# Down projection of a gated feed-forward: where its raw weight tiles lie and in which order its loads are issued

## The chip, the core and the metric

The kernel runs on one core of a Trainium2 chip. Its time is the device time of one execution in microseconds, and the value of a kernel is the median of its runs. A profile is one further execution with its own time.

Five engines work beside each other, each on its own instruction stream in a fixed order: TensorE (PE; its weight loads are listed as PEld), VectorE (DVE), ScalarE (ACT), GpSimd (POOL) and SyncE (SP). Here SP only issues DMAs. An issue that must wait, for a semaphore of another engine or for the landing of an earlier DMA, holds all issues behind it on the same engine. GpSimd issues a few DMAs too, on a queue of its own.

## The reference, cut to what matters

The reference is one layer of a streaming encoder: a mixer with three kinds of recurrent heads, then a convolutional feed-forward, each between two norms, for a prompt of 1024 tokens and a sample of 32. The change touches the feed-forward:

```
def conv_ffn(xn, buf, w_up, conv_w, conv_b, w_down):
    up = xn @ w_up                                   # 1024 -> 2 * 2816
    up, buf = causal_dwconv(up, buf, conv_w, conv_b) # 3 taps along time
    gate, val = jnp.split(up, 2, axis=-1)
    return (jax.nn.gelu(gate, approximate=True) * val) @ w_down, buf
...
        h, ffn_buf = conv_ffn(rms_norm(x, g_ffn_pre[l]), states[6][l], ...)
        x = x + rms_norm(h, g_ffn_post[l])
```

All of it is in 32-bit floats.

## The kernel before

**Products.** Each 32-bit operand is split into a high part (a cast by ScalarE, L93) and a remainder (a subtraction by VectorE, L94); a product is three matmuls, high by high, high by low and low by high (`mm3`, L87 to L90). Both feed-forward projections are done as seven block products instead of eight (Strassen-like sums of blocks, called p1 to p7 and P1 to P7).

**Up projection.** `up_all` (L1483) goes over NF = 22 feature tiles f of 128. For each, `up_block` makes gate and value columns for all tokens in two buffers `uu`, and `up_finish` (L1411) applies the three taps, the gelu and the product of both halves, and stores the gated tile, 128 x 1024, to the DRAM tensor `h_d[f]` (L1424, issued by SP). The last product of the last tile multiplies S3 by T3. The operands T2, T3 and T4 and the buffers y, uu and the kept products lie in pools of the right side of the on-chip memory that are closed after it (L1959 to L1962).

**Down projection.** `down_all` (L1613) then computes the seven products in the order P2, P1, P4, P6, P5, P7, P3. Each `run` (L1627) goes over NP = 11 steps p. P2 pairs rows `h_d[11+p]` with the raw weight tile `w_dn[11+p]`, and P1 rows `h_d[p]` with `w_dn[p]`. A step of P2 or P1 casts and splits one half of the row tile (`P2h`, `P1h`; four buffers) and of the raw tile (`P2w`, `P1w`; seven buffers) and does 12 matmuls into four banks. After steps 3, 7 and 9 `sample_products` (L1604) multiply the sample's rows by the raw tiles of steps 0 to 3, 4 to 7 and 8 to 10.

**Its loads.** `down_raw` (L1555) loads a raw tile, 128 x 1024 floats, 512 KB. It deals P2's and P1's tiles, in the order in which they are asked for, to nine buffers: two of a pool that the up projection used (`praw[0]`), five of the pool `ph` on the left side, opened when the last up tile begins (`freed`, L1929), and two of the pool p11 (`praw[2]`). So P2's tiles 0 and 1 take the first two, 2 to 6 the next five, 7 and 8 those of p11, and P2's 9 and 10 and P1's 0 and 1 come again to the buffers of P2's 0 to 3, which the sample products after step 3 read last. `load_h` (L1575) loads a row tile, also 512 KB; all 22 keep their own bytes to the end, rows 11 to 21 in `ph`, rows 0 to 10 in p11. `freed` asks for P2's raws 0 to 3 and rows 11 to 13; the rest is asked for by `rows_of` (L1686), which is called after each step: in P2 rows 14 to 21 after steps 0 to 7 and rows 0 to 5 after steps 5 to 10; in P1 rows 6 to 10. A raw tile from 4 on is asked for when its step's operands are made.

**Where p11 lies.** p10, with the accumulators CA, CB and the output norm's gain `gp`, and p11 are opened on the right side after the up projection's pools close. In p11 tiles lie in the order in which they are first asked for: row 0 at byte 124544 of each partition, row 1 at 128640, the two raw buffers at 132736 and 136832, rows 2 to 10 from 140928. The three y buffers of `up_finish` lay at 127232, 131328 (which holds the last gated tile) and 135424; T3's two parts from 139520 to 155904, then T2 and T4. A tile waits for the readers and writers of the tiles whose bytes it takes.

**What sets the order.** The framework's scheduler orders each engine's instructions by program order, as far as what they depend on has been scheduled. `with tc.issue_after(x)` puts an instruction behind x on the same engine's queue, with no semaphore. `behind["SP"]` holds the raw load that was traced last; `load_h` is put behind it.

Of the kernel before, what the change touches and what calls it, by code (L numbers as in the profile page):

```python
# [8 lines left out]
F32 = mybir.dt.float32  # L9
# [3 lines left out]
AF = mybir.ActivationFunctionType  # L13
# [5 lines left out]
SEQ = 1024  # L19
# [3 lines left out]
NF = DFF // 128  # L23
# [55 lines left out]
def body(ctx: ExitStack, tc: tile.TileContext, a: dict):  # L79
    nc = tc.nc  # L80
    act, dve, pool, pe, sp = nc.scalar, nc.vector, nc.gpsimd, nc.tensor, nc.sync
# [41 lines left out]
    h_d = dr.tile([NF, 128, SEQ], F32, name="h_d")  # L123
# [115 lines left out]
    cols_of, dcs_of, behind = {}, {}, {}  # L239
# [1171 lines left out]
    def up_finish(py, f, uu):  # L1411

        ys = []
        for i, j in enumerate((f, NF + f)):
            u = uu[i][:, 2:]
            y = py.tile([128, SEQ], F32, tag="y", name=f"y{j}", bufs=3)
            behind["POOL"] = pool.tensor_copy(fhalo[:, j, :], u[:, SEQ - 2:SEQ])  # L1417
            act.activation(y, u, AF.Identity, scale=fconv[:, j, 2:3], bias=fconv[:, j, 3:4])  # L1418
            for s in range(2):
                dve.scalar_tensor_tensor(y, uu[i][:, s:s + SEQ], fconv[:, j, s:s + 1], y, op0=ALU.mult, op1=ALU.add)  # L1420
            ys.append(y)
        act.activation(ys[0], ys[0], AF.Gelu_apprx_tanh)
        dve.tensor_tensor(ys[0], ys[0], ys[1], op=ALU.mult)
        sp.dma_start(h_d[f], ys[0])  # L1424

    def up_samples():

# [55 lines left out]
    def up_all(pw_, W0, X, uus, py, freed, ahead, begun):  # L1483
# [4 lines left out]
        for f in range(NF):  # L1488
# [3 lines left out]
            for s in (0, 1) if f == 0 else (None,):  # L1492
                if s != 0:
                    blk = up_block(pw_, f, s, W[f], X, uu)
                    next(blk)
                    next(late, None)
                    m = (2 * f + (1 if s is None else s) - 3) * len(SUMS) // 34
                    while len(summed) < min(m, len(SUMS)):
                        sum_weights(*SUMS[len(summed)])
                        summed.append(m)  # L1500
                    if f:
                        up_finish(py(), f - 1, uus[(f - 1) % len(uus)])
                        W.pop(f - 1)
                    next(blk)
                    if f == NF - 1:
                        freed()
                else:
                    blk = begun
                if s != 0 and f + 1 < NF:
                    ops = up_operands(f + 1, raw.pop(f + 1))  # L1510
                    W[f + 1] = next(ops)
                    for _ in ops:
                        pass
                yield
                if f:
                    next(rounds, None)
                next(blk)
                late = blk
                if f > len(UGROUPS) * (len(VISITS) + 1):
                    next(rounds, None)  # L1520
                yield
        for _ in rounds:
            pass
        ahead()
        next(late, None)
        up_finish(py(), NF - 1, uus[(NF - 1) % len(uus)])

    praw, ph, EARLY = [], [], 3

    NP = NF // 2  # L1530
# [21 lines left out]
    wraws = {}  # L1552
    VISITS_D = {3: range(4), 7: range(4, 8), NP - 2: range(8, NP)}

    def down_raw(kind, p):  # L1555

        key = (kind, p if kind in ("P1", "P2") else p // 2)
        if key in wraws:
            return
        n = len(wraws) % (9 if kind in ("P1", "P2") else 7)  # L1560
        pool_, bufs = (praw[0], 2) if n < 2 else (ph[0], 5) if n < 7 else (praw[2], 2)
        r = pool_.tile([128, 2, 512], F32, tag="raw", name=f"wr{kind}_{p}", bufs=bufs)
        if kind in ("P1", "P2"):
            f = p + NP * (kind == "P2")
            behind["SP"] = sp.dma_start(r.rearrange("p j n -> p (j n)"), a["w_dn"][f])
        else:
            n = min(2, NP - p)
            src = a["w_dn"][NP + p:NP + p + n, :, 512:].rearrange("f p n -> p f n") if kind == "P3" else \
                ws_d[{"P5": 0, "P7": 1, "P6": 2, "P4": 3}[kind]][:, p:p + n, :]
            behind["SP"] = sp.dma_start(r[:, :n, :], src)  # L1570
        wraws[key] = r

    hts = {}

    def load_h(pool_, f):  # L1575
        hts[f] = pool_.tile([128, SEQ], F32, name=f"ht{f}")
        with tc.issue_after(behind["SP"].ins):
            sp.dma_start(hts[f], h_d[f])

    def ablk(i, k, p):  # L1580
        h = hts[p + NP * k]
# [9 lines left out]
    def down_operands(ph, kind, p, early=False):  # L1591
        down_raw(kind, p)
        late = tc.issue_after(kept["w"].ins) if kind == "P1" and p else ExitStack()
        with late:
            h = halves_of(ablk(*ASRC[kind], p), f"{kind}h{p}", ph, "hop", 4)
        wp = (ph, "hop", 4) if early else (praw[1], "op", 7)
        if kind in ("P1", "P2"):
            r = wraws[kind, p]
            w = halves_of(r[:, 0], f"{kind}w{p}", *wp)
        else:  # L1600
            w = halves_of(wraws[kind, p // 2][:, p % 2], f"{kind}w{p}", *wp)
        return h, w

    def sample_products(ps, k, qs):  # L1604

        with tc.issue_after(behind["PE"].ins):
            for q in qs:
                for j in range(2):
                    r = 64 * (q % 2) + DEC * j
                    pe.matmul(ps[r:r + DEC], smp_h[:, q + NP * k, :], wraws["P2" if k else "P1", q][:, j],  # L1610
                              start=q < 2, stop=q >= NP - 2)

    def down_all(ph, pc, begun, late):  # L1613
# [1 line left out]
        CA = pc.tile([128, 4, 2, 512], F32, name="ca")  # L1615
        CB = pc.tile([128, 4, 2, 512], F32, name="cb")
        gp = pc.tile([128, 1024], F32, name="gp")
        sp.dma_start(gp, a["grows"][1:2, :].broadcast_to([128, 1024]))
        act.activation(gp[:, 512:], gp[:, 512:], AF.Copy, scale=-1.0)
        ssp = late.enter_context(tc.tile_pool(name="p11", bufs=1, side="right", reuse_waits="tile"))  # L1620
        praw.append(ssp)

        def w_banks(name):
            return [psf.tile([128, 512], F32, tag="sx", name=f"{name}0", bufs=1)] + \
                [psb.tile([128, 512], F32, tag="big", name=f"{name}{i}", bufs=3) for i in range(1, 4)]
# [60 lines left out]
        def rows_of(k, bank, first=lambda: None):  # L1686

            banks = []

            def each(p, w):  # L1690
                if p == 1:
                    first()
                if p in VISITS_D:
                    if p == NP - 2:
                        down_raw("P2" if k else "P1", p + 1)
                    banks.append(banks[0] if banks else bank())
                    sample_products(banks[0], k, VISITS_D[p])
                if k:
                    for f in (NP + EARLY + p, p - NP + 6):
                        if 0 <= f < NF and f not in hts:  # L1700
                            load_h(ph if f >= NP else ssp, f)
                elif p + 6 < NP:
                    load_h(ssp, p + 6)
            return each

        def sample_bank(pool_, tag, name, bufs):
# [7 lines left out]
        srow = []  # L1714
        W = w_banks("q2")
        run("P2", W, True, True, rows_of(1, lambda: sample_bank(psf, "xw", "s1", 4)))
        keep = pc.tile([128, 512], F32, name="keep")
        act.copy(keep, srow[0])
        X = [psf.tile([128, 512], F32, tag="xw", name=f"x{i}", bufs=4) for i in range(4)]
        run("P1", X, True, False, rows_of(0, lambda: sample_bank(psb, "big", "s2", 3), leave_q2))  # L1720
        dve.tensor_tensor(keep, keep, srow[1], op=ALU.add)
        quarter = pc.tile([DEC, 3, 512], F32, name="quarter")
# [206 lines left out]
    def freed():  # L1929
        pxs.close()  # L1930
        ph.append(phs.enter_context(tc.tile_pool(name="ph", bufs=1, side="left", reuse_waits="tile")))
        for p in range(EARLY):
            down_raw("P2", p)
            load_h(ph[0], NP + p)
        down_raw("P2", EARLY)
# [26 lines left out]
    p3s.close()  # L1962
    p10 = p8s.enter_context(tc.tile_pool(name="p10", bufs=1, side="right", reuse_waits="tile"))
    down_all(ph[0], p10, begun, late)
    late.close()
    p8s.close()
# [135 lines left out]
```

## Time and profile before

| what | value |
|---|---|
| time, median of 3 runs | 1357.03 us (1356.63 to 1359.81) |
| the profiled execution: its time | 1357.25 us |
| its span, first to last instruction | 1355.3 us |
| mean granted TensorE clock | 0.984 |
| PE, DVE, ACT, POOL busy | 96%, 75%, 52%, 23% |
| DMA | 291.73 MB, mean 215 GB/s |
| loads of P2's and P1's raw tiles (L1565) | 22, of 512 KB, 1094.1 to 1172.2 us |
| loads of row tiles (L1578) | 22, of 512 KB, 1103.3 to 1150.8 us |

Times in the trace are microseconds from the first instruction. A line of the timeline has the start, the duration, the engine, the kernel's line, the operation, what it writes and reads, and in brackets how long the engine stood idle before it and what ended that. Numbers of tiles are left out there (`ht` for ht3, `wrP` for wrP2_7), and neighbours of one kind are merged: "x4" with 1.76 us is four issues within that time. "SPq" is an issue by SP. The tables of stretches give busy time by engine, the clock granted to TensorE (1.00 is full), the mean busy share of the 16 DMA engines and what they moved in GB/s. Matmuls are pipelined: one is listed with 0.39 us, and they start about 0.227 us apart.

### The profile page before, as it was taken

What the parts mean: (1) busy time and instruction counts of PE and PEld (TensorE: products, weight loads), DVE (VectorE), ACT (ScalarE), POOL (GpSimd) and SP (SyncE); (2) the same over time, 40 slices, a digit from 0 to 9 for tenths busy, and PEclk for the clock granted to TensorE, in tenths of its full rate; (3) what the DMA queues carried; (4) which work ended last, traced back from release to release, by engine and by line L of the source; (5) the groups of instructions that cost most, each with busy time, mean ns of one, the idle gap of its engine ahead of it and who ended that gap; (6) DMA issues with size and microseconds to landing.
All of it is one profiled execution on the core that took longest, in us unless ns stands there. A gap on an engine that the chain in (4) does not pass through costs nothing.

```text
span 1355.3 us, 25578 instructions
## 1 busy us (share of the span) xinstructions
PE 1303.5 (96%) x9896; PEld 1101.9 (81%) x9896; DVE 1013.6 (75%) x1748; ACT 698.1 (52%) x1298; POOL 309.1 (23%) x412
## 2 busy tenths in 40 slices
PE   6999999998999999999899999999999997999997
PEld 6999889998888877777787777777788885778885
DVE  5796659768598778865888777697898874499566
ACT  5555555564575555434754544445355543454552
POOL 4532302145032243222100101141411000020005
PEclk9999999999998999989999999999999998999999
DMA  9799878886789864443537887877574259544335
GB/s 344 239 356 375 276 239 269 266 288 196 285 236 342 305 205 147 137 149 119 172 114 210 258 239 221 259 181 217 124 186 126 93 201 374 204 165 139 136 94 124
DMA packets 134784, 291.73 MB, mean 215 GB/s; under 512 B 29015, under 2 KB 63991, under 8 KB 132535
## 3 DMA queue, kind: packets, MB, share of 16 engines
q1 hardware_dynamic: 121031, 267.03, 58.3%
q0 software_dynamic: 9120, 18.62, 7.7%
q10 hardware_dynamic: 4512, 4.46, 1.0%
q8 instruction: 77, 1.26, 0.4%
q14 instruction: 44, 0.36, 0.1%
HBM read 229.38 MB, written 85.78 MB: 233 GB/s over the span
## 4 chain that ended last, share of the span: by engine, by line
PE 63%; DVE 8%; DMA 2%; ACT 2%; issue 2%; POOL 1%; DVEq 0%; POOLq 0%; SPq 0%; ACTq 0%
PE pux_None L88 4%; PE pux_None L90 4%; PE pux_None L89 4%; PE puw_None L88 3%; PE puw_None L90 3%; PE puw_None L89 3%; PE q L88 2%; PE q L89 2%; PE q L90 2%; PE x L88 2%; PE x L90 2%; PE x L89 2%; PE zp L90 2%; PE zp L88 2%; PE zp L89 2%; PE us L1451 2%
## 5 line engine op out<-in xcount | busy, mean ns | idle before, releaser
L1420 DVE SCALAR_TENSOR_TENSOR y<-uu,fconv_sb,y 128x1024 f32<-128x1024 f32 x88 | 117.9, 1340 | 27.0 <-ACT y L1418 26.5
L1417 POOL COPY fhalo<-uu 128x2 f32<-128x2 f32 x44 | 17.3, 392 | 364.2 <-DVE uu L1336 352.6
L88 PE MATMUL pv<-wt_0h,xh 128*128 128x256 f32 (+1 forms) x192 | 56.1, 292 | 3.1 <-DVE xl L319 1.9
L90 PE MATMUL zp<-woh,cl 128*128 128x512 f32 (+1 forms) x144 | 57.5, 399 | 1.5 <-DVE cl L1091 1.5
L1418 ACT ACTIVATE y<-uu,fconv_sb 128x1024 f32<-128x1024 f32 x44 | 54.8, 1245 | 7.6 <-DVE uu L1336 7.1
L88 PE MATMUL zp<-woh,ch 128*128 128x512 f32 (+1 forms) x144 | 56.9, 405 | 1.0 <-ACT ch L1090 0.8
L89 PE MATMUL zp<-wol,ch 128*128 128x512 f32 (+1 forms) x144 | 57.4, 399 | 0.3 <-DVE wol L94 0.3
L90 PE MATMUL pv<-wt_1h,xl 128*128 128x256 f32 (+1 forms) x192 | 55.1, 287 | 0.0
L90 PE MATMUL pv<-wt_0h,xl 128*128 128x256 f32 (+1 forms) x192 | 54.8, 286 | 0.0
L88 PE MATMUL pv<-wt_1h,xh 128*128 128x256 f32 (+1 forms) x192 | 54.8, 285 | 0.0
L1666 POOL TENSOR_TENSOR gss<-gss 128x1 f32<-128x1 f32 (+1 forms) x9 | 9.4, 1048 | 197.9 <-ACT gjk L1659 197.9
L89 PE MATMUL pv<-wt_0l,xh 128*128 128x256 f32 (+1 forms) x192 | 54.6, 284 | 0.0
L89 PE MATMUL pv<-wt_1l,xh 128*128 128x256 f32 (+1 forms) x192 | 54.5, 284 | 0.0
L206 POOL TENSOR_SCALAR hrs<-hss 128x5 f32<-128x5 f32 (+3 forms) x27 | 10.1, 375 | 174.8 <-DVE hss L1000 171.9
L816 DVE COPY_PREDICATED P<-masks_sb,sc 128x352 f32<-128x352 int32 (+3 forms) x53 | 37.7, 712 | 5.7 <-PE sc L729 5.0
L88 PEld LDWEIGHTS pv<-wt_0h,xh 128*128 128x128 f32 x192 | 36.2, 188 | 4.8 <-DVE xl L319 2.3
L207 POOL TENSOR_TENSOR hrs<-hrs,mhalf 128x5 f32<-128x5 f32 (+3 forms) x27 | 37.2, 1377 | 2.2
L88 PEld LDWEIGHTS pv<-wt_1h,xh 128*128 128x128 f32 x192 | 36.3, 189 | 0.7 <-issue 0.6
L1000 DVE TENSOR_REDUCE hss<-sq 128x5 f32<-128x320 f32 (+3 forms) x27 | 13.6, 502 | 30.8 <-ACT sq L999 30.8
L89 PEld LDWEIGHTS pv<-wt_0l,xh 128*128 128x128 f32 x192 | 36.3, 189 | 0.2
L90 PEld LDWEIGHTS pv<-wt_0h,xl 128*128 128x128 f32 x192 | 36.2, 189 | 0.2
L90 PEld LDWEIGHTS pv<-wt_1h,xl 128*128 128x128 f32 x192 | 36.1, 188 | 0.3
(1898 smaller groups left out, 4685.5 us busy)
## 6 DMA issues: line engine op xcount, KB each, us to landing
wus<-in_w_us SPq DMA_DIRECT2D x16, 1024.0 KB, 7.8
wrP<-in_w_dn SPq DMA_DIRECT2D x27, 512.0 KB, 3.7
h_d<-y SPq DMA_DIRECT2D x22, 512.0 KB, 4.5
ht<-h_d SPq DMA_DIRECT2D x22, 512.0 KB, 8.9
wt_0r<-in_w_tok SPq DMA_DIRECT2D x21, 512.0 KB, 5.2
wt_1r<-in_w_tok SPq DMA_DIRECT2D x21, 512.0 KB, 6.3
ws_d<-in_w_dn POOLq DMA_DIRECT2D x20, 512.0 KB, 7.3
wrP<-ws_d SPq DMA_DIRECT2D x20, 512.0 KB, 3.9
```

Source lines behind the costliest of these rows:

```text
L88: pe.matmul(ps, lh[0], rh[0], start=first, stop=False, **kw)
L89: pe.matmul(ps, lh[0], rh[1], start=False, stop=False, **kw)
L90: return pe.matmul(ps, lh[1], rh[0], start=False, stop=last, **kw)
L206: pool.tensor_scalar(out, ss, 1.0 / width, eps, op0=ALU.mult, op1=ALU.add)
L207: pool.tensor_tensor(out, out, mhalf[:n, :cols], op=ALU.pow)
L816: dve.copy_predicated(dst, mk.broadcast_to([n, 11, *mk.shape[2:]]), src)
L1000: dve.tensor_reduce(ss[:n, h0:h0 + nh], sq3, axis=mybir.AxisListType.X, op=ALU.add)
L1417: behind["POOL"] = pool.tensor_copy(fhalo[:, j, :], u[:, SEQ - 2:SEQ])
L1418: act.activation(y, u, AF.Identity, scale=fconv[:, j, 2:3], bias=fconv[:, j, 3:4])
L1420: dve.scalar_tensor_tensor(y, uu[i][:, s:s + SEQ], fconv[:, j, s:s + 1], y, op0=ALU.mult, op1=ALU.add)
L1451: pe.matmul(ps[DEC * q:DEC * q + DEC], smp_x[:, k, :], wus[:, i % RING_S, q, :], start=k == 0, stop=k == 7)
L1666: pool.tensor_tensor(ss[:n, 0:1], ss[:n, 2:3], ss[:n, 3:4], op=ALU.add)
```

## The change

Five edits around the first two products of the down projection:

- Rows 0 to 3 get their bytes in p11 before the raw buffers do. So the two raw buffers lie at 140928 and 145024, rows 2 and 3 at 132736 and 136832; the rest stays.
- Each raw load of P2 and P1 is put behind the raw load asked for before it, and `load_h` now sets `behind["SP"]` too, so row loads follow each other as well.
- After step 3 of P2 all raws 4 to 10 are asked for at once, alternating with rows 17 to 20, then row 21. Rows 14 to 16 are asked for after steps 0 to 2 as before.
- Rows 0 to 5 are asked for after steps 7 (row 0), 8 (1, 2), 9 (3, 4) and 10 (5). `gp`'s load, with ScalarE's instruction on it, comes after step 9, behind the row load before it, instead of at the start of `down_all`.
- The last gated tile is stored by GpSimd instead of SP.

```
-        sp.dma_start(h_d[f], ys[0])
+        (pool if f == NF - 1 else sp).dma_start(h_d[f], ys[0])
...
-            behind["SP"] = sp.dma_start(r.rearrange("p j n -> p (j n)"), a["w_dn"][f])
+            with ExitStack() as order:
+                if wraws:
+                    order.enter_context(tc.issue_after(behind["raw"].ins))
+                behind["raw"] = behind["SP"] = sp.dma_start(r.rearrange("p j n -> p (j n)"), a["w_dn"][f])
...
+    def place_h(pool_, f):
+        hts[f] = pool_.tile([128, SEQ], F32, name=f"ht{f}")
+
+    loaded = set()
+
     def load_h(pool_, f):
-        hts[f] = pool_.tile([128, SEQ], F32, name=f"ht{f}")
+        if f in loaded:
+            return
+        loaded.add(f)
+        if f not in hts:
+            place_h(pool_, f)
         with tc.issue_after(behind["SP"].ins):
-            sp.dma_start(hts[f], h_d[f])
+            behind["SP"] = sp.dma_start(hts[f], h_d[f])
...
-        sp.dma_start(gp, a["grows"][1:2, :].broadcast_to([128, 1024]))
-        act.activation(gp[:, 512:], gp[:, 512:], AF.Copy, scale=-1.0)
         ssp = late.enter_context(tc.tile_pool(name="p11", bufs=1, side="right", reuse_waits="tile"))
         praw.append(ssp)
+        for f in range(4):
+            place_h(ssp, f)
...
+                if k and p == 3:
+                    for q in range(p + 1, NP):
+                        down_raw("P2", q)
+                        if q < 8:
+                            load_h(ph, NP + EARLY - 1 + q)
                 if k:
-                    for f in (NP + EARLY + p, p - NP + 6):
-                        if 0 <= f < NF and f not in hts:
-                            load_h(ph if f >= NP else ssp, f)
+                    if p < 3:
+                        load_h(ph, NP + EARLY + p)
+                    if p == 3:
+                        load_h(ph, NF - 1)
+                    for f in {7: (0,), 8: (1, 2), 9: (3, 4), 10: (5,)}.get(p, ()):
+                        load_h(ssp, f)
                 elif p + 6 < NP:
                     load_h(ssp, p + 6)
+                if k and p == 9:
+                    with tc.issue_after(behind["SP"].ins):
+                        sp.dma_start(gp, a["grows"][1:2, :].broadcast_to([128, 1024]))
+                    act.activation(gp[:, 512:], gp[:, 512:], AF.Copy, scale=-1.0)
```

## The prediction

> **What bounds the kernel now.** I read the page first, then a table of stretches around the down projection, then the timeline of each engine there. The page's first part says who is busy:
>
> ```profile
> PE 1303.5 (96%) x9896; PEld 1101.9 (81%) x9896; DVE 1013.6 (75%) x1748; ACT 698.1 (52%) x1298; POOL 309.1 (23%) x412
> ```
>
> TensorE bounds it, so a change here is worth what it takes out of TensorE's idle time or slow clock. The stretches (length, then busy time of each engine, the granted clock, the share of the DMA engines and GB/s) show where that is:
>
> ```profile
> 1104.00:1125.00 21.00, 21.00 (x97) 17.13 (x99) 16.16 (x20) 10.94 (x17) 0.77 (x2) 1.00 1.00 387
> 1125.00:1128.00 3.00, 3.00 (x22) 1.37 (x22) 3.00 (x5) 1.14 (x2) 0.00 (x0) 1.00 0.57 153
> 1128.00:1160.00 32.00, 25.15 (x111) 17.34 (x110) 10.53 (x17) 11.58 (x21) 0.00 (x0) 0.89 1.01 395
> 1160.00:1300.00 140.00, 140.00 (x635) 111.65 (x634) 99.78 (x161) 67.44 (x126) 8.06 (x5) 1.00 0.44 141
> 1220.00:1250.00 30.00, 30.00 (x134) 24.84 (x133) 30.00 (x51) 14.41 (x26) 0.00 (x0) 1.00 0.44 119
> ```
>
> TensorE is full on both sides and idle for 6.85 us between 1128 and 1160, where the clock also falls to 0.89. The DMA engines are full for almost the whole of products P2 and P1 (1104 to 1160) and half idle just before the gap. TensorE's timeline shows the gap:
>
> ```profile
> 1132.42 1.07 PE L88 MATMUL q<-P2w,P2h 128*128 128x512 f32 x4
> ...
> 1134.91 0.39 PE L90 MATMUL q<-P2w,P2h 128*128 128x512 f32 x1
> 1142.15 2.07 PE L88 MATMUL q<-P2w,P2h 128*128 128x512 f32 x4 [6.85 <-ACT P2w L93]
> ...
> 1147.44 1.92 PE L1610 MATMUL s<-wrP,smp_h 128*32 128x512 f32 x16
> ...
> 1156.80 0.50 PE L88 MATMUL q<-P2w,P2h 128*128 128x512 f32 x1
> ...
> 1159.69 0.39 PE L88 MATMUL x<-P1w,P1h 128*128 128x512 f32 x1
> ```
>
> A step of P2 is 12 matmuls; in step 6 they start 1132.42 to 1134.91, 11 spacings of 0.227 us, so a step is 2.72 us. Step 7 starts at 1142.15 because of the weight operand P2w. ScalarE, which casts it, was itself waiting:
>
> ```profile
> 1117.58 0.59 ACT L1331 COPY c_21None<-pux_None 128x512 f32<-128x512 f32 x1
> ...
> 1132.62 0.62 ACT L93 CAST P2h<-ht 128x512 fp32r<-128x512 f32 x1 [1.58 <-PE q L90]
> 1136.88 0.63 ACT L1619 ACTIVATE gp<-gp 128x512 f32<-128x512 f32 x1 [3.64 <-DMA gp<-in_grows]
> 1141.48 0.62 ACT L93 CAST P2w<-wrP 128x512 fp32r<-128x512 f32 x1 [3.96 <-DMA wrP<-in_w_dn]
> ```
>
> It waited first for gp, then for raw tile 7. SP's queue of issues tells why that tile was late:
>
> ```profile
> 1116.08 0.33 SPq L1565 DMA_DIRECT2D wrP<-in_w_dn  x1
> 1117.40 0.32 SPq L1578 DMA_DIRECT2D ht<-h_d  x1
> 1119.23 0.34 SPq L1957 DMA_DIRECT2D out_p_fc<-fhalo  x1
> 1126.05 1.76 SPq L1565 DMA_DIRECT2D wrP<-in_w_dn  x4
> 1127.89 0.47 SPq L1424 DMA_DIRECT2D h_d<-y  x1
> 1128.42 0.44 SPq L1618 DMA_DIRECT2D gp<-in_grows  x1
> 1128.91 7.08 SPq L1578 DMA_DIRECT2D ht<-h_d  x2
> 1136.03 0.43 SPq L1565 DMA_DIRECT2D wrP<-in_w_dn  x1
> ```
>
> The issue at 1116.08 is the seventh raw tile, P2 6. The four at 1126.05 are not 7 to 10. By L1560 and L1561 P2 7 and 8 use the late pool p11, while P2 9, 10 and P1 0, 1 reuse the buffers of P2 0 to 3, which the sample products read; the queue's own waits name those:
>
> ```profile
> SPq L1565 <- PE s L1610: 16.7, 3, 6.7
> SPq L1578 <- DMA h_d<-y: 6.2, 1, 6.2
> ```
>
> So the four early ones are 9, 10, P1 0 and P1 1; P2 7 is the issue at 1136.03. It stands behind the store of gated tile 21, gp, h0 and h1, and h1 held SP 6.2 us until that store had landed, because h1's bytes in p11 overlap the buffer being stored. Raw 7's bytes (in the program's layout 132736 to 136832 of a partition) overlap that same buffer (131328 to 135424), so it could not have gone earlier either.
>
> **Part by part.** *Raw tiles on other bytes.* Placing h0 to h3 first moves the two raw buffers of p11 up by two tiles, to 140928 and 145024. There lie only T3h and T3l (139520 to 155904), whose last reader is the last up-projection product; ScalarE copies its result at 1117.58. So raws 7 and 8 wait for nothing after 1117.6 instead of the store's landing.
>
> *Raws chained, rows chained.* Raw 9 may no longer overtake 7 and 8, and rows 17 to 20 alternate with raws 4 to 7. The order on SP becomes raw 6, h19, (out_p_fc), raw 7, h20, raw 8, raw 9, raw 10, h21, then h0 on. Raw 7 takes the place of an issue at 1117.40 or, behind out_p_fc, 1119.6. Rows and raws landed in:
>
> ```profile
> DMA to landing us min/median/max: 3.6/8.9/11.4
> ```
>
> (that of the rows). Even 11.4 us gives 1131.0; raw 8 one 0.524 MB tile later, at 395 GB/s 1.33 us, 1132.3. Without the gap step 7 starts at 1134.91 + 0.227 = 1135.14, step 8 at 1137.86. Raw 9 still waits for the sample products until 1126.05 and holds SP, but nothing needed before step 9 is now behind it. The half-idle 1125 to 1128 is filled by raws 7 and 8.
>
> *Sum for the gap.* 1142.15 - 1135.14 = 7.01 us. Step 7 then took 1147.44 - 1142.15 = 5.29 us at the lower clock instead of 2.72: 2.57 us. Together **9.58 us**. Everything after 1147.44 moves up by that: step 10 from 1156.80 to 1147.22, P1 from 1159.69 to 1150.11. From 1160 to 1300 TensorE is full at clock 1.00, so nothing there gives the time back unless a load fails to move up too. VectorE, full from 1220 to 1250, works on TensorE's releases and moves with it.
>
> *Last store by GpSimd.* GpSimd has no work from 1125 to 1160 (0.00 above), so nothing waits behind the store; row 21's load waits for it. No store of this size by GpSimd is in the trace; its nearest rows are its accumulating copies, issue and landing:
>
> ```profile
> L1547 POOL DMA_DIRECT2D ws_d<-in_w_dn x24: 845/1158/1809, 732.4 to 1044.5; - x24
> ...
> DMA to landing us min/median/max: 4.2/7.2/9.9
> ```
>
> The tile is ready by VectorE, and its subtraction shows what a cast still needs:
>
> ```profile
> 1126.28 1.22 DVE L1423 TENSOR_TENSOR y<-y,y 128x1024 f32<-128x1024 f32 x1
> 1127.41 0.68 DVE L94 TENSOR_TENSOR P2h<-ht,P2h 128x512 fp32r<-128x512 f32 x1
> ```
>
> at 1127.50, so the store lands between 1131.7 and 1137.4; SP's own would land at the 1135.1 at which h1 was released. I take 1134.7 (the median). Row 21 then needs 3.6 to 11.4 us: 1138.3 to 1146.1. It must be there by 1147.22 - 0.62 - 0.68 = 1145.9. Behind few transfers the short end is nearer, so no stall; both long ends together would cost 1137.4 + 11.4 - 1145.9 = 2.9 us. SP is held at row 21 instead of h1, with h0 and P1's loads behind it.
>
> *Next rows later, gp later.* h0 to h5 and gp no longer stand ahead of raws 7 and 8. But P1 now wants them 9.58 us sooner, so the bandwidth must be checked. Before P1's step 2 can start the DMA engines must move, from 1104: the 16 tiles of before up to 1128 (rows 11 to 20, raws 2 to 6, one store), then raws 7 to 10, row 21, the store, gp, P1's raws 0 to 2 and h0 to h7, 18 more. At 387 GB/s until 1128 they have moved 17.7 of the 34; 16.3 x 1.33 us = 21.7, 1149.7, plus 0 to 3 us of idle DMA while row 21 waits: 1149.7 to 1152.7. Step 2 of P1 starts at 1150.11 + 5.44 = 1155.55, so its operands must land by 1154.25. Margin 1.5 to 4.5 us, taken as no stall. gp's ScalarE instruction moves behind the wait for its load: gp lands six tiles after row 21, at 1138.3 + 6 x 1.33 = 1146.3. With it wait the casts queued behind it. Were these P1's very first two, they would be done at 1146.3 + 0.63 + 2 x 0.62 + 0.68 = 1148.9, before 1150.11, so I cost it at nothing; with row 21 at its late end (1146.1) the same order would cost 6.6 us, and P1's casts from step 2 on, wanted 5 us later, 1 us.
>
> The profiled execution took 1357.25 us (span 1355.3), 0.2 above the median of 1357.03. 1357.25 - 9.58 = 1347.67; against the median 1357.03 - 9.58 = **1347.5 us**.
>
> **A rule against a row.** In an earlier gap TensorE stood still for less than 3 us:
>
> ```profile
> 508.38 0.63 PE L1086 MATMUL ctp<-ident,ct 128*128 128x128 f32 x4 [2.52 <-DMA ct<-cat_d]
> ...
> 509.00:512.00 3.00, 3.00 (x9) 2.34 (x8) 1.97 (x6) 1.56 (x4) 0.83 (x1) 0.50 0.69 272
> ```
>
> After 2.52 us idle the next 3 us ran at clock 0.50, which costs 1.5 us on top. The Trainium skill ("TensorE: Matmul & The Clock Gate", Part 1) has the clock fall only after an idle window of about 3.4 us; by it a leftover stall of 2.5 us would cost 2.5, by this row 4.0. The row decides, and the second case below uses it.
>
> **The rivals.**
> *The loads of P1 or row 21 come late (0.22).* For: the margin of 1.5 us, DMA engines at 1.01. Against: two late ends must meet. A stall of 1 to 3 us, with up to 1.5 for the clock, costs 1 to 4.5 us: 1348.5 to 1352.0; only with gp ahead of P1's first casts as well 6.6, 1354.
> *Raw 7 is not issued sooner (0.07).* If SP's order still puts it behind row 21's wait for the store, the load is at about 1135 as before: 1357. Against: the chain puts h20 and row 21 behind raw 7.
> *Slower: the GpSimd store lands very late (0.04).* SP then stands at row 21 with all of P1's loads behind it. P1 would have to begin after 1159.69 + 4.1 = 1163.8, so step 10 after 1161.1 (at full clock), row 21 after 1159.8, the store landed after 1156.2 at 3.6 us for the row: from then on it is slower than before. With the store at 1159 the time is about 1364. That is 31 us for a store; the 24 issues above needed at most 9.9. The Trainium skill ("SBUF — State Buffer", SBUF: two separate sides) says that some VectorE instructions lock GpSimd out while it writes its DMA descriptors, and advises the other queues. The trace shows VectorE's instructions here at 0.68 to 1.22 us each, so even one such wait is small.
>
> **How the numbers follow.** My forecast has 0.65, the three rivals 0.22, 0.07 and 0.04, and 0.02 stays for more than the gap gives. A measurement of this kernel tells about 0.3% (4.1 us) from no change. Faster takes the first two and the last, nearly all: 0.87; the same 0.09; slower 0.04. The range goes from 1346.0 (1.5 below, the runs of before differing by up to 3.2 us) to the end of the second case, 1352.0, and leaves out little more than a tenth.
>
> **What would show it.** Right: raw 7 issued before 1121, three raws ahead of raw 9's wait, no line with 6.85 at L88, clock 1.00 from 1128 to 1160, P1's first matmul near 1150.1, SP's wait for the store now at row 21. Wrong: a gap on TensorE before P2's step 10 or in P1's first four steps, ended by row 21, a P1 raw or ScalarE's gp; or raw 7 still issued after 1130.

## The result, and the profile after

The changed kernel took 1351.67 us (median of 6 runs, 1350.80 to 1355.77), the kernel before on the same chip 1359.14 us (6 runs, 1356.63 to 1362.85). The ratio is 0.9947, with a 95% interval of 0.9926 to 0.9968: some 7.5 us faster, where 9.6 were forecast. The profiled execution took 1355.77 us with a span of 1354.0, the slowest of the six. This matters for reading it: TensorE reached product P2 5.4 us later than in the profile of before (1116.67 against 1111.26), with other short stalls in the recurrent heads, which the change doesn't touch. In the profiles of this study P2 begins anywhere from 1106 to 1117 us. So the lengths below are counted from P2's first matmul on, each from one profiled execution.

| us from the first matmul to that of a later product | before | after | forecast |
|---|---|---|---|
| P2 to P1 | 48.43 | 40.86 | 38.85 |
| P1 to P4 | 36.27 | 36.42 | |
| P2 to the end | 244.04 | 237.33 | 234.46 |

(The forecasts are 1150.11 - 1111.26 and 244.04 - 9.58.)

The stretches of the kernel after, columns as before:

```profile
1128.00:1160.00 32.00, 30.29 (x150) 20.48 (x149) 14.36 (x22) 13.00 (x24) 0.61 (x1) 1.00 0.89 339
1136.00:1140.00 4.00, 4.00 (x19) 3.32 (x18) 2.58 (x5) 2.42 (x5) 0.00 (x0) 1.00 0.41 167
```

TensorE's 25.15 us of 32 became 30.29, and its clock is 1.00 instead of 0.89. The idle stretch of the DMA engines moved: it is now 1136 to 1140, while row 21 waits for the store. SP's issues and the waits of its queue in the kernel after:

```profile
1124.64 0.34 SPq L1981 DMA_DIRECT2D out_p_fc<-fhalo  x1
1125.07 0.38 SPq L1568 DMA_DIRECT2D wrP<-in_w_dn  x1
1125.50 0.42 SPq L1590 DMA_DIRECT2D ht<-h_d  x1
1126.34 5.92 SPq L1568 DMA_DIRECT2D wrP<-in_w_dn  x3
1140.21 3.90 SPq L1590 DMA_DIRECT2D ht<-h_d  x6
1144.15 0.46 SPq L1726 DMA_DIRECT2D gp<-in_grows  x1
1144.66 0.46 SPq L1590 DMA_DIRECT2D ht<-h_d  x1
1145.22 0.56 SPq L1568 DMA_DIRECT2D wrP<-in_w_dn  x1
```

```profile
SPq L1590 <- DMA h_d<-y: 8.6, 2, 7.9
SPq L1568 <- PE s L1622: 3.8, 1, 3.8
```

The order is the forecast one (the line of the loads of row tiles is now L1590, that of the raw tiles L1568): behind out_p_fc come raw 7 (1125.07), h20, raws 8, 9 and 10 (within 1126.34 to 1132.26, raw 9 held 3.8 us by the sample products), then row 21 at 1140.21, which held SP for 7.9 us until the store had landed. Rows 0 to 4, gp, row 5 and P1's raw 0 (1145.22) follow. GpSimd's part is one line:

```profile
1133.21 0.61 POOL L1424 DMA_DIRECT2D h_d<-y  x1 [8.60 <-DVE y L1423]
```

The 6.85 us gap at P2's step 7 is gone. What is left on TensorE is one gap, ahead of P1, and ScalarE's timeline shows what it waited for:

```profile
1157.53 1.20 PE L88 MATMUL x<-P1w,P1h 128*128 128x512 f32 x4 [1.71 <-ACT P1w L93]
```

```profile
1152.88 0.59 ACT L1742 COPY keep<-s 128x512 f32<-128x512 f32 x1 [5.92 <-PE s L1622]
1153.82 2.62 ACT L1736 COPY ca<-q 128x512 f32<-128x512 f32 x4 [0.35 <-PE q L90]
1156.33 0.63 ACT L1727 ACTIVATE gp<-gp 128x512 f32<-128x512 f32 x1
1156.87 0.61 ACT L93 CAST P1w<-wrP 128x512 fp32r<-128x512 f32 x1
```

In the kernel before, ScalarE had cast P1's first two raw tiles long before their product began at 1159.69:

```profile
1146.80 1.13 ACT L93 CAST P1w<-wrP 128x512 fp32r<-128x512 f32 x2
```

Now the first of them comes behind the copy of the sample's sums, four copies of P2's banks and gp's instruction, although its load had landed at 1155.65 by the records of the landings, 1.22 us before its cast at 1156.87.

### The profile page after: what moved, and what is told of

The parts are those of the page before. It is cut to its first block, busy times and chain, and to the rows that moved or that the text cites. A ratio compares the mean times of both kernels' runs of the same rounds, so it can differ in the third digit from the quotient of the medians.

```text
span 1354.0 us, 25583 instructions
## 1 busy us (share of the span) xinstructions
PE 1302.9 (96%) x9896; PEld 1100.6 (81%) x9896; DVE 1013.6 (75%) x1748; ACT 697.0 (51%) x1298; POOL 311.1 (23%) x413
## 3 DMA queue, kind: packets, MB, share of 16 engines
q8 instruction: 77, 1.26, 0.4%
## 4 chain that ended last, share of the span: by engine, by line
PE 60%; DVE 7%; DMA 4%; ACT 3%; issue 2%; POOL 1%; ACTq 0%; SPq 0%; DVEq 0%; POOLq 0%
PE pux_None L88 4%; PE pux_None L90 4%; PE pux_None L89 4%; PE puw_None L89 3%; PE puw_None L88 3%; PE puw_None L90 3%; PE q L88 2%; PE q L90 2%; PE q L89 2%; PE x L90 2%; PE x L88 2%; PE x L89 2%; PE zp L90 2%; PE zp L88 2%; PE zp L89 2%
## 5 line engine op out<-in xcount | busy, mean ns | idle before, releaser
L90 PE MATMUL zp<-woh,cl 128*128 128x512 f32 (+1 forms) x144 | 57.5, 399 | 1.5 <-DVE cl L1091 1.5
L90 PE MATMUL pv<-wt_1h,xl 128*128 128x256 f32 (+1 forms) x192 | 55.4, 289 | 0.0
L90 PE MATMUL pv<-wt_0h,xl 128*128 128x256 f32 (+1 forms) x192 | 54.4, 283 | 0.0
L90 PEld LDWEIGHTS pv<-wt_1h,xl 128*128 128x128 f32 x192 | 36.3, 189 | 0.3
L89 PEld LDWEIGHTS pv<-wt_1l,xh 128*128 128x128 f32 x192 | 36.3, 189 | 0.1
L1004 POOL TENSOR_TENSOR cat<-cat,gt 128x320 f32<-128x320 f32 (+3 forms) x27 | 30.3, 1124 | 24.9 <-DVE cat L1002 24.7
```

The lines of the kernel that those rows point to most:

```text
L89: pe.matmul(ps, lh[0], rh[1], start=False, stop=False, **kw)
L90: return pe.matmul(ps, lh[1], rh[0], start=False, stop=last, **kw)
L1004: pool.tensor_tensor(cat[:n, c0:c0 + 64 * nh], cat[:n, c0:c0 + 64 * nh], gt[:n, c0:c0 + 64 * nh], op=ALU.mult)
```

## The experiments

Two questions were put. Which of the five edits removes the gap at step 7? And what makes the new gap of 1.71 us ahead of P1? The first theory was the prediction's: raw 7 needs the new bytes and the new order, and the store's engine matters little. Its rivals were that the order alone does it, or the bytes alone, or the store. For the new gap the theories were P1's late loads, ScalarE's order, and gp. All lengths below are between first matmuls in the profiled execution of each kernel; each experiment's own kernel is shown by its difference to the kernel after or before:

| kernel | P2 to P1 | P1 to P4 | P2 to the end | gap ahead of step 7, of P1 |
|---|---|---|---|---|
| before | 48.43 | 36.27 | 244.04 | 6.85, 0 |
| after | 40.86 | 36.42 | 237.33 | 0, 1.71 |
| after, again | 40.86 | 36.42 | 236.66 | 0, 1.71 |
| after, store by SP | 40.86 | 36.42 | 236.88 | 0, 1.71 |
| after, old bytes | 42.12 | 38.03 | 239.58 | 0, 2.96 |
| after, gp in P1 | 40.34 | 36.41 | 236.14 | 0, 1.19 |
| after, P1's raws ahead of row 21 | 38.99 | 36.26 | 235.40 | 0, 0 |
| after, ScalarE's order | 39.41 | 36.94 | 235.73 | 0, 0.26 |
| before, new bytes | 48.06 | 36.26 | 243.66 | 6.41, 0 |
| before, store by GpSimd | 47.78 | 36.27 | 243.44 | 6.04, 0 |
| before, raws chained | 41.97 | 36.27 | 237.56 | 2.40, 0 |

**The kernel after with the last store by SP.**

```
-        (pool if f == NF - 1 else sp).dma_start(h_d[f], ys[0])
+        sp.dma_start(h_d[f], ys[0])
```

> The changed kernel with the last gated tile stored by SP again; everything else of the change stays. In SP's order the store then stands between out_p_fc and raw 7. Theory (the order of the loads and the bytes carry the gain, the store's engine little): raw 7 is issued when gated tile 21 is ready, about 16.5 us after P2's first matmul, lands 4 to 6 us later, so just in time for step 7 (24 us after P2's first matmul); from P2's first matmul to P1's first 41 to 43 us (before 48.4, changed 40.9), ratio to before about 0.995. Rival (the store on GpSimd's queue is what lets raw 7 go): a gap of 3 us or more ahead of step 7, 45 us or more, ratio 0.997 to 1.000.

It took 1349.93 us (12 runs; before on that chip 1355.90, 26 runs), ratio 0.9964 (0.9947 to 0.9981). Both products have the length that they have in the kernel after, so the 41 to 43 us that were expected were a little too many. SP's issues in this kernel, then ScalarE's cast of raw 7:

```profile
1130.76 0.32 SPq L1424 DMA_DIRECT2D h_d<-y  x1
1131.17 0.38 SPq L1568 DMA_DIRECT2D wrP<-in_w_dn  x1
```

```profile
1135.76 0.62 ACT L93 CAST P2w<-wrP 128x512 fp32r<-128x512 f32 x1 [2.01 <-DMA wrP<-in_w_dn]
```

Here SP waits for VectorE's last gated tile, and raw 7 is issued behind the store, at 1131.17. Counted from P2's first matmul (1114.49) that is 16.7 us, 8.3 later than in the kernel after. It is still in time: its cast begins 21.3 us after P2's first matmul, and step 7 is due at 23.9 (the forecast's 1135.14 - 1111.26). So the store by GpSimd is not needed.

**The kernel after with the raw buffers on their old bytes.**

```
-        for f in range(4):
+        for f in range(2):
             place_h(ssp, f)
```

> The changed kernel, but only rows 0 and 1 get their bytes first, so the raw buffers of p11 lie where they lay before, over the buffer of gated tile 21. Theory (the bytes are needed): raw 7 waits for the store of tile 21 to land, about 23 us after P2's first matmul, with row 20, raws 8 to 10 and row 21 held behind it on SP, so a gap of 4 to 8 us ahead of step 7 and more waits behind it; from P2's first matmul to P1's first 47 to 55 us, ratio 0.999 to 1.005. Rival (the order of the loads alone carries the gain): no gap ahead of step 7, 41 us, ratio 0.995.

It took 1352.55 us (12 runs, the same runs of before), ratio 0.9971 (0.9952 to 0.9990). From this kernel's timeline GpSimd's store, SP's issue of raw 7, ScalarE's cast of it and TensorE's first matmul of P1, and then two stretches:

```profile
1133.88 0.61 POOL L1424 DMA_DIRECT2D h_d<-y  x1 [8.60 <-DVE y L1423]
```

```profile
1136.86 0.33 SPq L1568 DMA_DIRECT2D wrP<-in_w_dn  x1
```

```profile
1140.38 0.62 ACT L93 CAST P2w<-wrP 128x512 fp32r<-128x512 f32 x1 [3.78 <-DMA wrP<-in_w_dn]
```

```profile
1159.45 1.54 PE L88 MATMUL x<-P1w,P1h 128*128 128x512 f32 x4 [2.96 <-ACT P1w L93]
```

```profile
1160.00:1164.00 4.00, 4.00 (x12) 3.15 (x11) 2.02 (x4) 1.36 (x3) 0.00 (x0) 0.57 1.03 421
1132.00:1137.00 5.00, 5.00 (x30) 3.43 (x23) 3.75 (x6) 0.90 (x2) 0.61 (x1) 1.00 0.26 105
```

Raw 7 does wait for the store, as the overlap of bytes demands. But nothing overtook it, so the DMA engines were three quarters idle (0.26) when the store came; it landed about 2.9 us after its issue at 1133.88, and raw 7 was cast 23.05 us after P2's first matmul, just in time for step 7 at 23.9. So the bytes are not needed at step 7 either, and the theory put on record for this run, a gap of 4 to 8 us there, failed. The bytes are worth something later: everything behind raw 7 on SP came later, P1 began after a gap of 2.96 us with half the clock behind it, and the two products together took 1.26 + 1.61 = 2.9 us more than in the kernel after. Here ScalarE's cast of P1's raw 0 waited for the load itself, which landed at 1158.76 by the records of the landings.

**The kernel before with one edit alone: the bytes.**

```
+        for f in range(4):
+            place_h(ssp, f)
```

(with `place_h` and the set of loaded rows as in the change, so that no row is asked for twice)

> The kernel before with one edit: rows 0 to 3 get their bytes first, so that P2's raws 7 and 8 lie over T3. Theory (SP's order decides, since raws 9, 10 and P1 0, 1 overtake raw 7 and row 1's wait for the store stands ahead of it): nothing changes, 48 to 49 us from P2's first matmul to P1's first (before 48.4, changed 40.9), the 6.85 us gap stays, ratio 0.999 to 1.001. Rival (the bytes carry the gain, as my prediction has it): raw 7 is issued at once, the gap shrinks to under 2 us, 40 to 42 us, ratio 0.995.

It took 1358.93 us (10 runs; before on that chip 1357.82, 13 runs), ratio 1.0004 (0.9984 to 1.0025). SP's issues in this kernel:

```profile
1126.57 1.76 SPq L1565 DMA_DIRECT2D wrP<-in_w_dn  x4
1128.42 0.44 SPq L1424 DMA_DIRECT2D h_d<-y  x1
...
1129.41 7.04 SPq L1585 DMA_DIRECT2D ht<-h_d  x2
1136.49 0.43 SPq L1565 DMA_DIRECT2D wrP<-in_w_dn  x1
```

Raw 7's bytes are free, but it stands where it stood, behind h1, which still waits for the store.

**The kernel before with one edit alone: the store.**

```
-        sp.dma_start(h_d[f], ys[0])
+        (pool if f == NF - 1 else sp).dma_start(h_d[f], ys[0])
```

> The kernel before with one edit: the last gated tile is stored by GpSimd. Theory: row 1 still holds SP until that store has landed, which is about 7 us while the DMA engines are full, as by SP: 48 to 49 us from P2's first matmul to P1's first, the gap within 1 us of 6.85. Rival (GpSimd's queue lets the store pass the four raws queued ahead of it, 3 us): the gap shrinks by 3 to 4.5 us, 43 to 45.5 us.

One run took 1357.06 us beside the same runs of before. The gap is 6.04 us. GpSimd's issue in this kernel, and SP's:

```profile
1128.39 0.61 POOL L1424 DMA_DIRECT2D h_d<-y  x1 [8.60 <-DVE y L1423]
```

```profile
1126.63 1.77 SPq L1565 DMA_DIRECT2D wrP<-in_w_dn  x4
...
1128.99 7.74 SPq L1578 DMA_DIRECT2D ht<-h_d  x2
1136.77 0.43 SPq L1565 DMA_DIRECT2D wrP<-in_w_dn  x1
```

By the records of the landings the store lands at 1136.35, still 8.0 us after its issue, behind the four raw tiles. h1, which waits for it, is the second of the two row loads and goes out at 1136.40.

**The kernel before with one edit alone: raw loads chained.**

```
-            behind["SP"] = sp.dma_start(r.rearrange("p j n -> p (j n)"), a["w_dn"][f])
+            with ExitStack() as order:
+                if wraws:
+                    order.enter_context(tc.issue_after(behind["raw"].ins))
+                behind["raw"] = behind["SP"] = sp.dma_start(r.rearrange("p j n -> p (j n)"), a["w_dn"][f])
```

> The kernel before with one edit: each raw load of P2 and P1 is put behind the raw load before it. Raws 9, 10, P1 0 and P1 1 then wait behind raw 7, and raw 7 still waits behind row 1 for the store by SP. Theory (the four overtaking raws are what delayed the store and raw 7): the store finds empty DMA engines and lands in about 3 us, raw 7 lands 23 to 25 us after P2's first matmul, the gap ahead of step 7 is 0 to 2 us, and with P1's loads late 40.5 to 44 us to P1's first, ratio 0.995 to 0.997. Rival (raw 7 must not wait for the store at all): the idle DMA time ahead of it costs as much as before or more, 47 us or more, ratio 0.999 or above.

It took 1351.87 us (4 runs, the same runs of before), ratio 0.9945 (0.9924 to 0.9965). From this kernel SP's issues, two gaps of TensorE (the first is far ahead of the change), and the stretches behind these two gaps:

```profile
1126.67 0.32 SPq L1424 DMA_DIRECT2D h_d<-y  x1
...
1127.52 2.33 SPq L1581 DMA_DIRECT2D ht<-h_d  x2
1129.89 0.43 SPq L1568 DMA_DIRECT2D wrP<-in_w_dn  x1
```

```profile
674.52 0.39 PE L88 MATMUL puw<-T1h,S_0h 128*128 128x256 f32 x1 [2.44 <-ACT T1h L1247]
...
1136.85 1.20 PE L88 MATMUL q<-P2w,P2h 128*128 128x512 f32 x4 [2.40 <-ACT P2w L93]
```

```profile
676.00:682.00 6.00, 4.91 (x18) 4.00 (x17) 5.93 (x9) 1.63 (x3) 0.00 (x0) 0.50 0.00 0
1137.00:1143.00 6.00, 6.00 (x34) 3.55 (x35) 2.51 (x4) 1.76 (x3) 0.00 (x0) 1.00 1.03 417
```

Raw 7 still stands behind the store, gp, h0 and h1, on its old bytes. But without four raw tiles ahead of it the store had landed by 1129.5, 2.9 us after its issue, so h1 held SP little and raw 7 was issued 19.5 us after P2's first matmul (1110.41 here) instead of 24.8. The gap shrank from 6.85 to 2.40 us (0 to 2 were expected), and the clock stayed at 1.00 behind it. This one edit, the raw half of the second of the five, gives 48.43 - 41.97 = 6.46 of the whole change's 7.57 us. The other 1.11 us, which are net of the new gap ahead of P1, were not split among the chain of the row loads, the earlier requests and the later rows.

**The kernel after with P1's raws 0 and 1 asked for ahead of row 21.**

```
                     if p == 3:
+                        for q in range(2):
+                            down_raw("P1", q)
                         load_h(ph, NF - 1)
```

> The changed kernel with P1's raw tiles 0 and 1 asked for right after P2's raw 10, ahead of row 21. In the changed kernel TensorE stands still 1.71 us ahead of P1's first step, and the DMA engines are at 0.41 and 0.57 while SP waits at row 21 for the store. Theory (P1's raw 0 comes late because it stands behind row 21's wait, rows 0 to 5 and gp): raws 0 and 1 fill the idle DMA time, ScalarE casts raw 0 before it copies P2's banks, no gap ahead of P1; from P2's first matmul to P1's first 39.0 to 39.3 us instead of 40.9, ratio 0.993 to 0.994. Rival (ScalarE's order, the copies of P2's banks and gp ahead of the cast, holds P1): the gap stays within 0.5 us of 1.71.

It took 1348.35 us (7 runs, the runs of before of the first kernel here), ratio 0.9937 (0.9910 to 0.9965). From this kernel's timeline SP's issues, ScalarE's casts of P1's first two raw tiles, and P1's first matmul:

```profile
1115.75 6.86 SPq L1568 DMA_DIRECT2D wrP<-in_w_dn  x5
1130.21 3.97 SPq L1590 DMA_DIRECT2D ht<-h_d  x6
```

```profile
1130.12 0.62 ACT L93 CAST P1w<-wrP 128x512 fp32r<-128x512 f32 x1 [0.52 <-DMA wrP<-in_w_dn]
1131.35 0.62 ACT L93 CAST P1w<-wrP 128x512 fp32r<-128x512 f32 x1 [0.61 <-DMA wrP<-in_w_dn]
```

```profile
1145.05 0.39 PE L88 MATMUL x<-P1w,P1h 128*128 128x512 f32 x1
```

Five raw tiles (P2's last three and P1's two) go out ahead of row 21's wait, and ScalarE casts P1's two 14 us before their product. No gap is left; P1 begins 38.99 us after P2, where the forecast had 38.85. So what made the gap hangs on the place of these two loads, either by their landing or by the order on ScalarE that follows from it; the run with ScalarE's order changed tells the two apart.

**The kernel after with gp's load and instruction after step 9 of P1 instead of P2.**

```
-                if k and p == 9:
+                if not k and p == 9:
```

> The changed kernel with gp's load and ScalarE's instruction on it asked for after step 9 of P1 instead of step 9 of P2. Theory (P1's raw 0 is late as a load): one tile less ahead of it, 1.3 us; the gap of 1.71 us ahead of P1 shrinks by 0.5 to 1.3. Rival (ScalarE is held by gp): the gap goes wholly or shrinks by the 0.6 us of gp's instruction only. If neither matters the gap stays at 1.71. From P2's first matmul to P1's first 39.2 to 40.4 us instead of 40.9, ratio 0.993 to 0.995.

It took 1348.11 us (8 runs, the same runs of before), ratio 0.9950 (0.9930 to 0.9970). The gap is 1.19 instead of 1.71, 0.52 less, about the spacing of one instruction on ScalarE (1156.33 to 1156.87 above). This run takes gp's load away too, and P1's raw 0 landed 37.9 instead of 39.0 us after P2's first matmul. But the gap shrank by half of that only, so it is ScalarE that P1 waited for, not the load. gp is a third of the gap, no more.

**The kernel after with ScalarE's order changed.** The four copies of P2's banks and gp's instruction are put behind the cast of P1's raw tile 1; no load is moved.

```
-                    act.activation(gp[:, 512:], gp[:, 512:], AF.Copy, scale=-1.0)
...
         def leave_q2():
-            for i in range(4):
-                act.copy(CA[:, i, 0], W[i])
+            with tc.issue_after(kept["w"].ins):
+                for i in range(4):
+                    act.copy(CA[:, i, 0], W[i])
+                act.activation(gp[:, 512:], gp[:, 512:], AF.Copy, scale=-1.0)
```

> The changed kernel with ScalarE's order altered and no load moved: the four copies of P2's banks and gp's instruction are put behind the cast of P1's raw 1. In the changed kernel they stand ahead of the cast of P1's raw 0, which had landed at 1155.65 and was cast from 1156.87. Theory (the gap of 1.71 us ahead of P1 is ScalarE's order first, the raw's landing close behind): the cast starts when raw 0 has landed, the gap shrinks to 0.3 to 0.8, 39.5 to 39.9 us from P2's first matmul to P1's first instead of 40.9, and no new gap of over 0.5 us behind it. Rival (the load alone holds P1): the gap stays at 1.4 or more.

It took 1349.65 us (4 runs; before 1357.82, 13 runs), ratio 0.9926 (0.9902 to 0.9951). ScalarE in this kernel:

```profile
1153.12 0.62 ACT L93 CAST P1w<-wrP 128x512 fp32r<-128x512 f32 x1 [1.94 <-DMA wrP<-in_w_dn]
...
1155.57 0.62 ACT L93 CAST P1w<-wrP 128x512 fp32r<-128x512 f32 x1 [1.31 <-DMA wrP<-in_w_dn]
1156.10 2.04 ACT L1736 COPY ca<-q 128x512 f32<-128x512 f32 x4
```

Now the cast waits for the load itself, and the gap is 0.26. So of the 1.71 us ScalarE's order made 1.45 (gp's 0.52 among it) and the load the rest. P1 to P4 became 0.52 longer, since the copies now stand ahead of the casts of P1's step 2, which begins 5.96 us after P1's first matmul instead of the two steps' 5.44: 1.45 gained, 0.52 given back.

**The change again, and both improvements together.** Three kernels on one chip: the kernel after unchanged; with P1's raws ahead of row 21 and gp in P1; and the same with the store by SP (the edits are those shown above).

> The changed kernel once more, beside the two below on the same chip. Its first profiled execution had its P2 begin 5.4 us later than before's, in parts of the kernel that the change does not touch. Theory: that is the spread between executions; from P2's first matmul to P1's first 40.7 to 41.0 us and to the end 236.5 to 237.5 us again (before 244.0), ratio 0.993 to 0.997. Rival (the change itself delays the earlier part): P2's first matmul again later than 1114.5.

> The changed kernel with P1's raws 0 and 1 ahead of row 21 and gp, load and instruction, after step 9 of P1. From P2's first matmul to P1's first 39.0 us (the 38.85 of my prediction's sum), no gap on TensorE down to the end, 234.5 to 235.2 us to the end, ratio 0.992 to 0.994. If gp's place still mattered beside the raws' it would be under 38.9; if moving gp behind P1's operands holds ScalarE in P1, a gap over 0.5 us between P1 and P4.

> The same with the last gated tile stored by SP. Theory (GpSimd's store is worth nothing once the raws are in order): within 0.3 us of the kernel above from P2's first matmul to P1's first and to the end, ratio 0.992 to 0.994. Rival (with P1's raws added behind raw 10, SP's wait for gated tile 21 makes raw 7 or row 21 late): a gap of over 0.5 us in P2, 39.5 us or more.

| kernel | median us (runs) | ratio (95%) | P2 to P1 | P2 to the end |
|---|---|---|---|---|
| before | 1357.99 (16) | | 48.43 | 244.04 |
| after, again | 1351.06 (11) | 0.9958 (0.9942 to 0.9974) | 40.86 | 236.66 |
| P1's raws first, gp in P1 | 1347.86 (6) | 0.9938 (0.9924 to 0.9951) | 38.99 | 234.64 |
| and the store by SP | 1348.50 (6) | 0.9934 (0.9919 to 0.9949) | 38.98 | 234.58 |

(The lengths of before are those of its profile above.) The second profile of the kernel after repeats the first: the same 40.86 and 36.42. Its P2 begins at 1113.08, 3.6 us earlier than in the first, so there was no delay of the earlier parts that came again. The first had P6 to P5 0.6 us longer than before (30.57 against 29.94), the second not (29.92), so that is spread. The two last kernels are 2.0 us shorter from P2 to the end than the change, and their medians are 2.6 to 3.2 us lower, though the intervals of the ratios overlap. The store by SP again changes nothing, and with P1's raws first, gp's place is worth at most the 0.3 us that is left of 235.40 - 234.64 after 30.42 - 29.93 of P6 to P5. So the kernels with the raws chained and early, P1's first two among them, are the shortest here from P2 to the end.

## Why the prediction was right, and where it was short

**The gap and its clock.** Right. The forecast moved step 10 from 45.54 to 35.96 us after P2's first matmul; it came at 36.09 (1152.76 - 1116.67). All of 7.01 + 2.57 us went, and the clock stayed at 1.00.

**SP's order.** Right to the last issue, with raw 7 8.4 us after P2's first matmul (forecast: before 9.7) and SP's long wait at row 21.

**GpSimd's store.** Right in size: 7.0 us from issue to landing by the records of the landings, where 7.2 was taken, and row 21 was cast 27.98 us after P2's first matmul, at the short end of the forecast's 27.0 to 34.8. Wrong in what sets it: the 7.2 came from other issues of GpSimd, but SP's own store shows the same range by what is queued ahead of it (last section), and the same store by GpSimd took 2.9 us with the old bytes. So that 7.2 came so near was luck. (SP's store in the kernel before landed at 1135.59; the prediction's 1135.1 is a misreading, on which nothing in its sum rests.) The rival in which it lands very late did not come.

**Next rows later, gp later: "taken as no stall".** This is the step that failed. The sum of bytes was made to step 2 of P1, and it held: after the first matmul nothing stalled. But it did not ask where P1's raw tile 0 stands among those 18 tiles. In the kernel before it was one of the four early ones; now it is the ninth load from row 21 on, issued 5.0 us after it (1145.22), and it is there at 1155.65, as P2's last matmuls run. The prediction's own numbers would have told: eight tiles behind a row 21 at 1138.3 it lands at 1138.3 + 8 x 1.33 = 1148.9 and is cast and split by 1150.2, when P1 was to begin at 1150.11. Step 0 had no margin where step 2 had 1.5 to 4.5 us. And the working of ScalarE's order was too short: gp's instruction was put ahead of P1's first casts, at a cost of nothing, but the four copies of P2's banks, each of which needs the last matmul into its bank, came ahead of them as well (2.62 us). That the scheduler put them there because the loads now come later is not shown by itself; it fits the kernel with P1's raws ahead, where the casts come long before the copies. The rival "the loads of P1 or row 21 come late" had the right place and the right size (1 to 3 us), though ScalarE's order made 1.45 of the 1.71. So one of the prediction's own signs of being wrong, a gap in P1's first four steps ended by a raw tile's cast, did come.

**Why raw 7 was late.** The prediction said that on its old bytes raw 7 "could not have gone earlier". It could, once the store itself lands sooner: the old bytes with the rest of the change have no gap at step 7, and the chain alone, on old bytes, takes off 4.45 us of it. What made it late was the landing time of the store, 7.7 us behind four raw tiles that were not wanted yet. Overtaking cost twice: the four tiles went ahead of raw 7, and they slowed the store for which raw 7's queue stood. Bytes alone and store alone leave 6.41 and 6.04 of 6.85.

**The rule against the row.** The row said that less than 3 us idle can halve the clock, the Trainium skill about 3.4. The gap of 2.96 us in the kernel with old bytes did halve it for about 3.4 us; the gap of 2.40 at step 7 did not, but one of 2.44 in the same execution, at 674.52, did (0.50 from 676 to 682). So the length alone doesn't decide. The same section of the Trainium skill ("TensorE: Matmul & The Clock Gate", Part 1) also says that the window in which activity is watched runs freely, not from the start of a kernel, so it matters where in it a gap falls; these rows agree with that, and not with the 3.4 us as a least gap. The traces say more. In their records of the clock every stretch at 0.50 lasts one, two or three times 3.413 us, except the last one at the kernel's end, and within one execution these stretches begin at multiples of 3.413 us from each other (in the kernel before, for example, at 676.20 and 1140.41, which are 136 times 3.413 apart). So each execution has a grid, and the table shows how that grid cuts six gaps. The first four gaps stand ahead of one and the same matmul of a recurrent head (L90, some 440 us from the start), which the change doesn't touch; the last two are those of the raws chained.

| kernel | gap ends at | gap | how the grid cuts it | clock from the next line of the grid on |
|---|---|---|---|---|
| after, again | 439.17 | 1.83 | 1.37 + 0.46 | 1.00 |
| after, old bytes | 442.21 | 1.82 | whole | 0.50 |
| P1's raws first, gp in P1, store by SP | 440.35 | 2.21 | 1.71 + 0.49 | 1.00 |
| P1's raws first, gp in P1 | 440.27 | 2.20 | whole | 0.50 |
| before, raws chained | 1136.85 | 2.40 | 1.65 + 0.75 | 1.00 |
| before, raws chained | 674.52 | 2.44 | whole | 0.50 |

In these rows a gap of 1.8 to 2.4 us halved the clock where it fell into one interval of the grid, and did not where a line of the grid cut it. Idle time is not all that counts: in the kernel before, the interval 171.02 to 174.44 shows no idle time of TensorE, only many small matmuls, and the next one ran at 0.50. What exactly the chip counts stays open.

**The number.** 1347.5 forecast; 0.9947 of the 1357.03 of then is 1349.8, and the median beside its own runs of before 1351.67. Both lie inside the range, but in the part of it (1348.5 to 1352.0) that was there for the first rival, whose chance was 0.22. So the mechanism of the forecast was right for the gap at step 7, and the number stayed in the range because the range took in a stall that the forecast itself put at nothing. The term of the sum that was missing is the 1.71 us ahead of P1, with 0.3 us of small change: 9.58 forecast, 7.57 measured to P1.

## What to carry to other kernels

When one load is late, look first at the queue that it is issued on: which issue at its head is waiting, what that one waits for, and which transfers not yet needed went ahead and fill the DMA engines; here one ordering rule did six sevenths of the work, and freed bytes alone gave 0.37 us to P1 and nothing measurable in the time. After moving loads back, follow the first tile of the next stage, not only the bytes up to its second step, and look on the casting engine for what will slip in ahead of a cast that now waits. Measure from a fixed point of the stage: the part ahead of it moved by up to 11 us between profiled executions, more than the change gave.

## What the runs showed of the hardware

The time that this 512 KB store needs, from issue to landing, went with what the DMA engines had queued, not with the engine that issued it: SP 2.9 us with the raws chained, and 7.7 behind four raw tiles (in the kernel before it was issued at 1127.89 and landed at 1135.59 by the records of the landings); GpSimd 2.9 us at a DMA share of 0.26, 7.0 in the kernel after and 8.0 behind the same four tiles. The Trainium skill ("DMA: Bandwidth & Descriptors", Issuing engines are not separate DMA queues) says that transfers run on the same 16 DMA engines whichever engine starts them; the runs agree, and moving this store to GpSimd changed 40.86 to 40.86.
